# Layer norm's scale and shift, and four low parts of weights, move from GpSimd to VectorE; the inverse's matrix products leave out columns that are zero or finished

## The chip, the cores and the metric

The kernel runs on one core of one Trainium2 chip. The metric is the device time of one execution in microseconds (us); three runs of the kernel before were timed, and one more execution was profiled. The engines are called as the profile calls them: PE is TensorE (matrix products; PEld its weight loads), DVE is VectorE, ACT is ScalarE, POOL is GpSimd and SP is SyncE, whose queue starts most transfers.

## The reference

256 latent tokens and 256 context tokens of width 1024 pass through two layers of three sub-layers: a gated feed-forward half-step, a mixer, and a second half-step. Each ends in a layer norm with a scale row `g` and a shift row `b`.

```python
def layer_norm(x, g, b):
    mu = jnp.mean(x32, axis=-1, keepdims=True)
    var = jnp.mean(jnp.square(x32 - mu), axis=-1, keepdims=True)
    return ((x32 - mu) * lax.rsqrt(var + NORM_EPS) * g + b).astype(x.dtype)
...
def ffn_sublayer(x, m, s, w_gu, w_down, g, b):
    shift, scale, gate = _mod(m, s)
    y = swiglu(x * (1 + scale) + shift, w_gu, w_down)
    return layer_norm(DEEP_ALPHA * x + FFN_HALF * gate * y, g, b)
...
    lmat = jnp.where(strict, jnp.einsum('bnhid,bnhjd->bnhij', kb, kc) * decay, 0.0)
    rhs = jnp.concatenate([vc * bc[..., None], kb * jnp.exp(gc)[..., None]], axis=-1)
    uw = lax.linalg.triangular_solve(lmat, rhs, left_side=True, lower=True, unit_diagonal=True)
```

Layer 0's mixer joins windowed attention (A) with a gated delta rule (B), which needs the triangular solve above; layer 1's mixer (C) is dense attention with rotary positions. In layer 1 only the latent tokens go on after the mixer.

## The kernel before

**Sub-layers.** They are numbered 0 to 5: `ffn(0)`, `ab_proj` and what follows it (sub-layer 1, mixer A and B), `ffn(2)`, `ffn(3)`, `mixer_c` (sub-layer 4) and `ffn(5)`. The stream `x` lies as four row blocks of 128 tokens x 1024 (buffers `r`; two latent, two context). The norm at the end of a sub-layer is split. Mean and variance are taken out of the rows at once (`norm_tb`), and the next sub-layer's products read transposed rows into whose per-channel factors `g` and `b` are folded. The rows themselves, which the next residual sum reads, are multiplied by `g` and shifted by `b` later, in the next sub-layer, by `affine_tb`: one multiplication (line 326) and one addition (line 328) of 128x1024 for each row block, both on POOL. These are 8 instructions for each of sub-layers 0, 1 and 2, and 4 for each of 3 and 4 (latent rows only): 32. For sub-layer 3 they are put off (`deferred`) to slot 4 of the attention of `mixer_c`.

**Weights.** Products are made from two parts of each operand. For a 128x1024 piece of weights, ACT rounds the raw weights `wr` into the high part `wh` (line 366), and an engine subtracts to get the low part `wl` (line 368, `split_w`): DVE, except for 12 pieces on POOL, among them the four query pieces of `ab_proj` (`need`, jobs with `c0 < 1280`). Each product is three matmuls: lines 383, 385 and 386 (`mm3`).

**A chunk of a half-step.** `ffn` goes over 22 chunks of 128 hidden channels, in parts of 8, 8 and 6. A chunk is 48 matmuls into two banks `pgu`, 256 columns each in `ffn(5)`, 512 elsewhere. Then ACT takes the silu (`sg`), DVE multiplies `sg` by the other bank (line 432), ACT rounds (`hhi`) and DVE subtracts (`hlo`, line 434). `next_fill` adds DVE work of the modulation vectors behind it (`acc`, line 169).

**`ab_proj`.** The projections of q, k, v each go through `ab_conv`, a five-tap convolution: one tap on ACT (line 897), four on DVE (`cacc`, line 908). Lines 826 to 847 are `scalars`, small operations on 128x32. The rows are stored away to `xs` by two POOL transfers (line 997).

**The inverse.** `delta_inverse` solves the triangular systems as 8 units of four 128x128 blocks, in pairs: `begin` makes a product `pN` with the solved diagonal blocks `AT` (line 1390), ACT copies it to `N` (tile `va`, line 1394); three `step`s make `pZ` (line 1403) from `N` and subtract on DVE (line 1408). All run over 128 columns. The inverse is woven between the slots of mixer A's attention (products `pS`, `pP`, `pOa`; `qs` comes from POOL, line 1290).

The order on each engine is settled by a scheduler when the program is built; instructions then wait for each other across engines.

Of the kernel before, what the change touches and what calls it, by code (L numbers as in the profile page):

```python
# [32 lines left out]
class Backbone:  # L33
    def __init__(self, ctx, tc, io):
# [363 lines left out]
    def ffn(self, sub, tail, lat_only=False, fill=()):  # L398
# [238 lines left out]
    def boundary(self, sub, streams=(0, 1), affine=(0, 1)):  # L637
# [6 lines left out]
        def rows(last):  # L644
            self.load_ln(sub)

            def apply():
                for j in affine:
                    for tb in (2 * j, 2 * j + 1):
                        self.affine_tb(tb, last)  # L650

            if sub == 3:
                self.deferred = apply
            else:
                apply()
# [280 lines left out]
    def ab_proj(self):  # L936
# [952 lines left out]
```

## Time and profile before

| | us |
| --- | --- |
| runs, lowest / median / highest of 3 | 1824.44 / 1825.21 / 1827.54 |
| the profiled execution, its own time | 1826.35 |
| its span in the trace | 1824.6 |
| busy: PE / PEld / DVE / ACT / POOL | 1758.4 / 1484.9 / 1264.7 / 672.8 / 290.7 |

The profiled execution is one run of its own, 1.14 us above the median of the timed ones; 1.75 us of its time lie outside the span. Busy times count an engine's instructions and not its waits. The granted clock of PE, 0.987 of full speed over the span, is shown in the windows as a share of full speed: 1.00 is 2.4 GHz, 0.50 is 1.2 GHz.

### The profile page before, as it was taken

Reading aid. Unit: us, or ns where it says so; the run is one execution under the profiler, and the core shown is the slowest. Engines: PE = TensorE matmul, PEld = TensorE weight load, DVE = VectorE, ACT = ScalarE, POOL = GpSimd, SP = SyncE. Lnnn points to the kernel's source line nnn. Section 1 sums busy time; section 2 is a strip of 40 time slices with the busy share of each in tenths; the row PEclk is TensorE's granted clock in tenths of the full one; section 3 lists DMA queues with packets and bytes.
Section 4 is the critical chain, followed back from the end, with each engine's and each line's share of the span. In section 5 each row is a group of like instructions: output and inputs, shape, how many; then the busy total and the mean of one; then the engine's idle time right before and its main releaser. Section 6 shows DMA issues by size and latency. Waiting matters only on the chain. (4 is left out here: it accounts for less than half of the span.)

```text
span 1824.6 us, 24388 instructions
## 1 busy us (share of the span) xinstructions
PE 1758.4 (96%) x9571; PEld 1484.9 (81%) x9571; DVE 1264.7 (69%) x1912; ACT 672.8 (37%) x1178; POOL 290.7 (16%) x324
## 2 busy tenths in 40 slices
PE   6999999999998999999999999999999999999997
PEld 2978878878787888877887888778878888878997
DVE  2774855867688986896673438976747769786556
ACT  2432331324664662332221323423332335634442
POOL 1000000017433210510000003400000046150000
PEclk8999999999998999999999999999999999999999
DMA  9563553522341213375552242664644433136552
GB/s 349 185 216 128 185 182 120 197 59 95 127 116 54 75 59 104 128 240 187 162 184 70 93 154 77 212 204 141 204 163 139 155 108 113 59 126 232 186 177 99
DMA packets 178173, 267.56 MB, mean 147 GB/s; under 512 B 14639, under 2 KB 126683, under 8 KB 177547
## 3 DMA queue, kind: packets, MB, share of 16 engines
q1 hardware_dynamic: 172944, 250.58, 41.4%
q0 software_dynamic: 4624, 14.29, 2.4%
q8 instruction: 75, 1.23, 0.3%
q10 hardware_dynamic: 491, 1.15, 0.2%
q14 instruction: 39, 0.32, 0.1%
HBM read 259.64 MB, written 6.34 MB: 146 GB/s over the span
## 5 line engine op out<-in xcount | busy, mean ns | idle before, releaser
L366 ACT ACTIVATE wh<-wr 128x1024 fp32r<-128x1024 f32 (+1 forms) x311 | 324.8, 1056 | 756.7 <-PE pdn L386 306.6
L368 DVE TENSOR_TENSOR wl<-wr,wh 128x1024 fp32r<-128x1024 f32 (+1 forms) x299 | 390.0, 1315 | 231.9 <-ACT wh L366 228.5
L383 PE MATMUL pgu<-ht_hi,wh 128*128 128x512 f32 (+1 forms) x1472 | 519.5, 355 | 14.7 <-DVE sg L432 8.4
L386 PE MATMUL pgu<-ht_hi,wl 128*128 128x512 f32 (+1 forms) x1472 | 520.4, 354 | 3.3 <-DVE wl L368 3.3
L385 PE MATMUL pgu<-ht_lo,wh 128*128 128x512 f32 (+1 forms) x1472 | 520.6, 355 | 1.0 <-POOL ht_lo L268 0.5
L383 PEld LDWEIGHTS pgu<-ht_hi,wh 128*128 128x128 f32 x1472 | 279.1, 191 | 57.8 <-DVE sg L432 10.9
L386 PEld LDWEIGHTS pgu<-ht_hi,wl 128*128 128x128 f32 x1472 | 280.4, 191 | 41.6 <-DVE wl L368 3.9
L385 PEld LDWEIGHTS pgu<-ht_lo,wh 128*128 128x128 f32 x1472 | 280.5, 191 | 39.1 <-POOL ht_lo L268 0.9
L169 DVE SCALAR_TENSOR_TENSOR acc<-wa,cv,acc 128x1024 f32<-128x1024 f32 x224 | 277.1, 1299 | 0.0
L385 PE MATMUL pdn<-wl,hhi 128*128 128x512 f32 (+1 forms) x622 | 241.1, 388 | 0.0
L383 PE MATMUL pdn<-wh,hhi 128*128 128x512 f32 (+1 forms) x622 | 239.9, 389 | 0.0
L386 PE MATMUL pdn<-wh,hlo 128*128 128x512 f32 (+1 forms) x622 | 239.6, 388 | 0.0
L383 PEld LDWEIGHTS pdn<-wh,hhi 128*128 128x128 f32 x622 | 116.7, 188 | 27.6 <-issue 2.5
L385 PEld LDWEIGHTS pdn<-wl,hhi 128*128 128x128 f32 x622 | 116.9, 188 | 23.7
L386 PEld LDWEIGHTS pdn<-wh,hlo 128*128 128x128 f32 x622 | 116.9, 188 | 23.6
L432 DVE TENSOR_TENSOR sg<-sg,pgu 128x512 f32<-128x512 f32 (+1 forms) x86 | 53.6, 623 | 108.6 <-PE pgu L386 105.1
L615 DVE SCALAR_TENSOR_TENSOR tm<-pdn,gate 128x512 f32<-128x512 f32 (+1 forms) x98 | 64.3, 675 | 60.0 <-PE pdn L386 59.8
L197 POOL DMA_DIRECT2D gsc<-rows x12 | 6.2, 525 | 615.3 <-DVE rows L180 615.3
L433 ACT ACTIVATE hhi<-sg 128x512 fp32r<-128x512 f32 (+1 forms) x86 | 49.7, 577 | 89.4 <-DVE sg L432 89.3
L431 ACT ACTIVATE sg<-pgu 128x512 f32<-128x512 f32 (+1 forms) x86 | 45.9, 534 | 59.6 <-PE pgu L386 59.6
L434 DVE TENSOR_TENSOR hlo<-sg,hhi 128x512 fp32r<-128x512 f32 (+1 forms) x86 | 59.8, 695 | 7.7 <-ACT hhi L433 7.7
L318 POOL TENSOR_TENSOR mv<-mv,mhalf 128x1 f32<-128x1 f32 x18 | 16.6, 932 | 272.3 <-DVE mv L317 272.3
(385 smaller groups left out, 2351.3 us busy)
## 6 DMA issues: line engine op xcount, KB each, us to landing
wr<-in_ffn_w_gu_dram SPq DMA_DIRECT2D x84, 1024.0 KB
wa<-in_ada_w_dram SPq DMA_DIRECT2D x144, 512.0 KB
wr<-in_ffn_w_down_dram SPq DMA_DIRECT2D x40, 1024.0 KB
wr<-in_ab_w_in_dram SPq DMA_DIRECT2D x11, 1024.0 KB
wr<-in_c_w_in_dram SPq DMA_DIRECT2D x6, 1024.0 KB
gate<-gsc POOLq DMA_DIRECT2D x10, 512.0 KB, 4.5
wr<-in_ffn_w_gu_dram SPq DMA_DIRECT2D x8, 512.0 KB
wr<-in_ffn_w_down_dram SPq DMA_DIRECT2D x8, 512.0 KB
```

The costliest lines, as they stand in the source:

```text
L169: i = nc.vector.scalar_tensor_tensor(out=acc[:, sl], in0=wa[:, sl], scalar=cv, in1=acc[:, sl], op0=ALU.mult, op1=ALU.add)
L318: nc.gpsimd.tensor_tensor(out=mv[:, 3:4], in0=mv[:, 2:3], in1=self.mhalf[:, 0:1], op=ALU.pow)
L366: self.last_high = nc.scalar.activation(out=hv, in_=raw, func=AF.Copy)
L368: self.last_split = (eng or nc.vector).tensor_tensor(out=lv, in0=raw, in1=hv.bitcast(F32), op=ALU.subtract)
L383: self.first_mm = nc.tensor.matmul(out=out, lhsT=lhs[0], rhs=rhs[0], start=start, stop=False)
L385: self.link(nc.tensor.matmul(out=out, lhsT=lhs[0], rhs=rhs[1], start=False, stop=False))
L386: self.last_mm = nc.tensor.matmul(out=out, lhsT=lhs[1], rhs=rhs[0], start=False, stop=stop)
L431: nc.scalar.activation(out=sg, in_=pts[0][:, :NT], func=AF.Silu)
L432: nc.vector.tensor_tensor(out=sg, in0=sg, in1=pts[1][:, :NT], op=ALU.mult)
L433: nc.scalar.activation(out=h_hi[:, c, :], in_=sg, func=AF.Copy)
L434: self.evacuated = nc.vector.tensor_tensor(out=h_lo[:, c, :], in0=sg, in1=h_hi[:, c, :].bitcast(F32), op=ALU.subtract)
L615: i = nc.vector.scalar_tensor_tensor(out=tm, in0=pt[:, cs], scalar=mul, in1=self.gate[:, t // 2, ds], op0=ALU.mult, op1=ALU.mult)
```

## The change

- The 32 scale-and-shift instructions go from POOL to DVE. `affine_tb` now only lists them (`self.affine`), and `next_affine` issues them behind a named DVE instruction: sub-layer 0's 8, two behind each query convolution of `ab_proj`; sub-layer 1's and 2's 8, two behind each of chunks 2 to 5 of the next half-step; sub-layer 3's 4, one in each of slots 2 to 5 of the attention of `mixer_c`; sub-layer 4's 4, two behind each of chunks 2 and 3 of `ffn(5)`.
- The low parts of the four query pieces of `ab_proj` are made on DVE.
- The two stores to `xs` are issued behind query convolutions 1 and 3, and the tile `vt` is allocated later.
- In the inverse, `pN` is made over 96 columns, and the three `pZ` over 96, 64 and 32; the DVE subtraction and ACT's copy shrink alike, and Z is written straight into `AT`. POOL gains, for each unit, a `memset` of 32 columns of `N` and a copy of 32 columns into `AT`: 16 instructions.

```diff
     def affine_tb(self, tb, after):
         nc = self.nc
         x = self.row_block(tb)
-        i = nc.gpsimd.tensor_tensor(out=x, in0=x, in1=self.lnr[:, 0, :], op=ALU.mult)
-        self.after(i, [after])
-        nc.gpsimd.tensor_tensor(out=x, in0=x, in1=self.lnr[:, 1, :], op=ALU.add)
+        lnr = self.lnr
+
+        self.affine += [
+            lambda i=i: nc.vector.tensor_tensor(out=x, in0=x, in1=lnr[:, i, :], op=(ALU.mult, ALU.add)[i]) for i in range(2)
+        ]
+
+    def next_affine(self, n, behind):
+
+        for _ in range(min(n, len(self.affine))):
+            self.after(self.affine.pop(0)(), [behind])
...
             self.next_fill()
+            if n == 0 and c > 1:
+                self.next_affine(2, self.evacuated)
...
-                eng = nc.gpsimd if c0 < 1280 else None
-                ws.append(self.split_w(raws[p][:, :, c0 - p:c0 - p + P], bool(ext), eng))
+                ws.append(self.split_w(raws[p][:, :, c0 - p:c0 - p + P], bool(ext)))
...
             if h == 1:
                 rows()
+            self.next_affine(2, self.convolved)
+            if h % 2:
+                nc.gpsimd.dma_start(out=self.xs[:, h - 1:h + 1], in_=self.rows[h // 2])
...
+            c0 = 0 if u < 4 else 32
             pN = self.bank("sc", "pN")
+            p3 = pN[:, 0:384].rearrange("p (t x) -> p t x", t=4)
             for tb in range(4):
                 nc.tensor.matmul(
-                    out=pN[:, tb * P:(tb + 1) * P], lhsT=self.AT[u][:, tb, :], rhs=x[:, tb, :], start=True, stop=True
-                )
-            N = self.tmp("va")
-            i = nc.scalar.activation(out=N, in_=pN, func=AF.Copy)
+                    out=p3[:, tb, :], lhsT=self.AT[u][:, tb, :], rhs=x[:, tb, c0:c0 + 96], start=True, stop=True,
+                )
+
+            N = cube(self.tmp("va"))
+            i = nc.scalar.activation(out=N[:, :, c0:c0 + 96], in_=p3, func=AF.Copy)
+            zc = 96 if u < 4 else 0
+            nc.gpsimd.memset(N[:, :, zc:zc + 32], 0.0)
...
+            dc = 0 if u < 4 else 96
+            nc.gpsimd.tensor_copy(out=self.AT[u][:, :, dc:dc + 32], in_=xT[:, :, dc:dc + 32])
...
+            w = 96 - 32 * it
+            c0 = 128 - w if u < 4 else 0
+            Z = xT if it == 0 else self.AT[u]
...
-            Zn = self.AT[units[n]] if it == 2 else cube(self.tmp("o"))
-            V.tensor_tensor(out=Zn, in0=xT, in1=cube(pZ), op=ALU.subtract)
-            state[n] = (xT, N, Zn)
+                    out=p3[:, tb, :], lhsT=N[:, tb, :], rhs=Z[:, tb, c0:c0 + w], start=True, stop=True,
+                )
+            V.tensor_tensor(
+                out=self.AT[u][:, :, c0:c0 + w], in0=xT[:, :, c0:c0 + w], in1=p3, op=ALU.subtract
+            )
...
-            if i == 4:
-                self.deferred()
+            if 1 < i < 6:
+                self.next_affine(1, self.weighted)
```

The rows that follow show the order on two engines; line numbers of the changed kernel are up to 19 higher. First DVE in `ffn(2)`, chunks 2 to 4 of the first part (`sg` and `hlo` end a chunk, `acc` is the fill behind it), before:

```order
L432 TENSOR_TENSOR sg<-sg,pgu_6964 128x512
L368 TENSOR_TENSOR wl<-wr,wh 128x1024 x2
L434 TENSOR_TENSOR hlo<-sg,hhi 128x512
L169 SCALAR_TENSOR_TENSOR acc_6923<-wa,cv,acc_6923 128x1024 x2
L169 SCALAR_TENSOR_TENSOR acc_6924<-wa,cv,acc_6924 128x1024 x2
L432 TENSOR_TENSOR sg<-sg,pgu_7034 128x512
L368 TENSOR_TENSOR wl<-wr,wh 128x1024 x2
L434 TENSOR_TENSOR hlo<-sg,hhi 128x512
```

The same place of the changed kernel (line 376 is `wl`, 440 `sg`, 442 `hlo`, 170 `acc`):

```order
L440 TENSOR_TENSOR sg<-sg,pgu_6956 128x512
L376 TENSOR_TENSOR wl<-wr,wh 128x1024 x2
L442 TENSOR_TENSOR hlo<-sg,hhi 128x512
L170 SCALAR_TENSOR_TENSOR acc_6915<-wa,cv,acc_6915 128x1024 x2
L170 SCALAR_TENSOR_TENSOR acc_6916<-wa,cv,acc_6916 128x1024 x2
L330 TENSOR_TENSOR r_6318<-r_6318,lnr 128x1024
L440 TENSOR_TENSOR sg<-sg,pgu_7028 128x512
L376 TENSOR_TENSOR wl<-wr,wh 128x1024 x2
L330 TENSOR_TENSOR r_6318<-r_6318,lnr 128x1024
L442 TENSOR_TENSOR hlo<-sg,hhi 128x512
```

The chunk has gained two instructions of line 330, one ahead of the next `sg` and one ahead of the next `hlo`. Next POOL in `ab_proj`, from the last `ht_lo` (the low parts of the transposed rows) to the store, before:

```order
L268 TENSOR_TENSOR ht_lo<-h_3148,ht_hi 128x256
L326 TENSOR_TENSOR r_91<-r_91,lnr 128x1024 x2
L326 TENSOR_TENSOR r_92<-r_92,lnr 128x1024 x2
L1160 MEMSET X 128x1024
L328 TENSOR_TENSOR r_91<-r_91,lnr 128x1024
L368 TENSOR_TENSOR wl<-wr,wh 128x1024
L328 TENSOR_TENSOR r_91<-r_91,lnr 128x1024
L368 TENSOR_TENSOR wl<-wr,wh 128x1024
L328 TENSOR_TENSOR r_92<-r_92,lnr 128x1024
L368 TENSOR_TENSOR wl<-wr,wh 128x1024
L328 TENSOR_TENSOR r_92<-r_92,lnr 128x1024
```

And of the changed kernel:

```order
L269 TENSOR_TENSOR ht_lo<-h_3148,ht_hi 128x256
L1165 MEMSET X 128x1024
L1166 MEMSET X 128x32
L938 TENSOR_TENSOR rk<-ssk,mhalf 128x16
L938 TENSOR_TENSOR rki<-ssk,phalf 128x16
L1029 DMA xs<-r_91 128x2048
L1029 DMA xs<-r_92 128x2048
```

POOL has nothing of 128x1024 with an input left there; the eleven instructions stand on DVE. Last POOL in the inverse (`qs` feeds the attention scores, `xv` loads the next units), before:

```order
L1368 MEMSET xv 128x2048
L1290 TENSOR_TENSOR qs<-qTa,qs 64x128 x3
L1377 DMA xv<-scr_in 32x4x32 x8
L1290 TENSOR_TENSOR qs<-qTa,qs 64x128 x3
L1377 DMA xv<-scr_in 32x4x32 x2
L1290 TENSOR_TENSOR qs<-qTa,qs 64x128 x3
```

And of the changed kernel:

```order
L1373 MEMSET xv 128x2048
L1405 MEMSET va 128x4x32
L1295 TENSOR_TENSOR qs<-qTa,qs 64x128 x3
L1382 DMA xv<-scr_in 32x4x32 x8
L1295 TENSOR_TENSOR qs<-qTa,qs 64x128 x3
L1410 COPY AT<-xv 128x4x32
L1405 MEMSET va 128x4x32
L1382 DMA xv<-scr_in 32x4x32
L1410 COPY AT<-z 128x4x32
L1382 DMA xv<-scr_in 32x4x32
L1295 TENSOR_TENSOR qs<-qTa,qs 64x128 x2
```

The `COPY` and `MEMSET` of a unit now stand ahead of some `qs` and `xv` in one queue.

## Rows read from the trace of the kernel before

**Rows 1.** The page of the profile: busy time of each engine, share of the span, instructions.
```profile
PE 1758.4 (96%) x9571; PEld 1484.9 (81%) x9571; DVE 1264.7 (69%) x1912; ACT 672.8 (37%) x1178; POOL 290.7 (16%) x324
```

**Rows 2.** The list of waits, engine PE, whole span: total us, times, longest us.
```profile
PE pgu L383 <- DVE sg L432: 8.4, 6, 2.0
...
PE pcT L1707 <- DVE kTlo L1712: 2.0, 1, 2.0
```

**Rows 3.** Groups by line and shape, DVE, 760 to 784 us: busy us, mean ns.
```profile
L368 DVE TENSOR_TENSOR wl<-wr,wh 128x1024 fp32r<-128x1024 f32 x4 | 12.9, 3268 | 0.0
L434 DVE TENSOR_TENSOR hlo<-sg,hhi 128x512 fp32r<-128x512 f32 x2 | 4.4, 2201 | 0.7 <-ACT hhi L433 0.7
...
L432 DVE TENSOR_TENSOR sg<-sg,pgu 128x512 f32<-128x512 f32 x2 | 1.3, 674 | 0.0
```

**Rows 4.** The same view, DVE, 805 to 840 us.
```profile
L169 DVE SCALAR_TENSOR_TENSOR acc<-wa,cv,acc 128x1024 f32<-128x1024 f32 x17 | 20.8, 1284 | 0.0
L368 DVE TENSOR_TENSOR wl<-wr,wh 128x1024 fp32r<-128x1024 f32 x8 | 9.7, 1224 | 0.0
...
L434 DVE TENSOR_TENSOR hlo<-sg,hhi 128x512 fp32r<-128x512 f32 x4 | 2.8, 689 | 0.0
```

**Rows 5.** The instructions of line 326: ns, first and last start.
```profile
L326 POOL TENSOR_TENSOR r<-r,lnr x16: 2405/2516/3384, 434.9 to 1629.7; 128x1024 f32<-128x1024 f32 x16
```

**Rows 6.** The timeline in sub-layer 2, PE: start us, length us, instruction.
```profile
797.19 0.51 PE L383 MATMUL pgu<-ht_hi,wh 128*128 128x512 f32 x1 [2.04 <-DVE sg L432]
...
798.50 0.63 PE L386 MATMUL pgu<-ht_hi,wl 128*128 128x512 f32 x1
...
801.89 0.40 PE L385 MATMUL pgu<-ht_lo,wh 128*128 128x512 f32 x1
...
802.59 0.40 PE L385 MATMUL pgu<-ht_lo,wh 128*128 128x512 f32 x1
```

**Rows 7.** The list of waits, engine PE, 1132 to 1190 us.
```profile
PE pgu L383 <- DVE sg L432: 3.9, 3, 2.0
```

**Rows 8.** The timeline in the query projections of `ab_proj`, DVE, ACT and PE.
```profile
457.25 2.42 DVE L834 TENSOR_SCALAR beta<-beta 128x32 f32<-128x32 f32 x1
...
460.25 1.79 DVE L830 SCALAR_TENSOR_TENSOR gu<-gy 128x32 f32<-128x32 f32 x1
...
462.07 0.23 ACT L831 ACTIVATE gu<-gu 128x32 f32<-128x32 f32 x1 [3.54 <-DVE gu L830]
...
464.91 0.66 PE L917 MATMUL pqt<-ident,sqT 128*128 128x128 f32 x4 [0.94 <-ACT sqT L912]
...
470.47 0.51 PE L383 MATMUL pproj<-ht_hi,wh 128*128 128x512 f32 x1 [3.32 <-ACT cacc L897]
```

**Rows 9.** Busy us by stretch: PE, PEld, DVE, ACT, POOL, clock, DMA share, GB/s.
```profile
460.00:480.00 20.00, 15.74 (x73) 12.79 (x72) 14.50 (x39) 11.85 (x37) 8.98 (x6) 0.91 0.60 211
600.00:640.00 40.00, 39.18 (x335) 35.27 (x334) 36.54 (x113) 26.98 (x87) 9.23 (x19) 1.00 0.25 84
1625.00:1645.00 20.00, 16.56 (x103) 14.66 (x102) 16.66 (x15) 6.73 (x12) 13.06 (x8) 0.91 0.21 63
```

**Rows 10.** The list of waits, engine PE, 1625 to 1665 us.
```profile
PE pgu L386 <- DVE wl L368: 3.3, 3, 2.3
PE pgu L383 <- ACT wh L366: 1.4, 1, 1.4
PE plead L386 <- DVE ht_lo L299: 0.8, 1, 0.8
```

**Rows 11.** The timeline of PE: a 128-column product of the inverse, a 32-column product.
```profile
591.28 1.06 PE L1403 MATMUL pZ<-o,va 128*128 128x128 f32 x8
592.09 0.48 PE L1298 MATMUL pS<-kk,qs 128*128 128x256 f32 x2
...
477.73 0.39 PE L859 MATMUL pgc<-gg,ones 128*128 128x32 f32 x2
477.95 0.64 PE L917 MATMUL pqt<-ident,sqT 128*128 128x128 f32 x4
```

More of the change, by code (lines that the diff above doesn't have):

```diff
@@ L46, in __init__ @@
         self.turn_at = 0
+        self.affine = []
     def new_ht(self):
@@ L645, in rows @@
             self.load_ln(sub)
[L647 to L655, printed above, removed]
+            for j in affine:
+                for tb in (2 * j, 2 * j + 1):
+                    self.affine_tb(tb, last)
         def context():
@@ L995, in ab_proj @@
         self.start_context()
-        for j in range(2):
-            nc.gpsimd.dma_start(out=self.xs[:, 2 * j:2 * j + 2], in_=self.rows[j])
         for n in range(4):
@@ L1039, in ab_proj @@
             self.ab_gram(h)
+            if h == 0:
+                self.vt = L.tile([P, 4, 4, P], F32, tag="gate", name="vt", bufs=1)
         self.ab_pow(self.rq, ssq, -0.5)
@@ L1387, in begin @@
             xT, x = (a, bt) if u < 4 else (bt, a)
+            c0 = 0 if u < 4 else 32
             pN = self.bank("sc", "pN")
+            p3 = pN[:, 0:384].rearrange("p (t x) -> p t x", t=4)
             for tb in range(4):
                 nc.tensor.matmul(
-                    out=pN[:, tb * P:(tb + 1) * P], lhsT=self.AT[u][:, tb, :], rhs=x[:, tb, :], start=True, stop=True
+                    out=p3[:, tb, :], lhsT=self.AT[u][:, tb, :], rhs=x[:, tb, c0:c0 + 96], start=True, stop=True
                 )
-            N = self.tmp("va")
-            i = nc.scalar.activation(out=N, in_=pN, func=AF.Copy)
+            N = cube(self.tmp("va"))
+            i = nc.scalar.activation(out=N[:, :, c0:c0 + 96], in_=p3, func=AF.Copy)
+            zc = 96 if u < 4 else 0
+            nc.gpsimd.memset(N[:, :, zc:zc + 32], 0.0)
             if n == 7:
                 self.mark = i
-            state[n] = (xT, N, xT)
+            dc = 0 if u < 4 else 96
+            nc.gpsimd.tensor_copy(out=self.AT[u][:, :, dc:dc + 32], in_=xT[:, :, dc:dc + 32])
+            state[n] = (xT, N)
         def step(n, it):
-            xT, N, Z = state[n]
+            u = units[n]
+            xT, N = state[n]
+            w = 96 - 32 * it
+            c0 = 128 - w if u < 4 else 0
+            Z = xT if it == 0 else self.AT[u]
             pZ = self.bank("sc", "pZ")
+            p3 = pZ[:, 0:4 * w].rearrange("p (t x) -> p t x", t=4)
             for tb in range(4):
                 nc.tensor.matmul(
-                    out=pZ[:, tb * P:(tb + 1) * P], lhsT=N[:, tb * P:(tb + 1) * P], rhs=Z[:, tb, :],
-                    start=True, stop=True,
-                )
-            Zn = self.AT[units[n]] if it == 2 else cube(self.tmp("o"))
-            V.tensor_tensor(out=Zn, in0=xT, in1=cube(pZ), op=ALU.subtract)
-            state[n] = (xT, N, Zn)
+                    out=p3[:, tb, :], lhsT=N[:, tb, :], rhs=Z[:, tb, c0:c0 + w], start=True, stop=True,
+                )
+            V.tensor_tensor(
+                out=self.AT[u][:, :, c0:c0 + w], in0=xT[:, :, c0:c0 + w], in1=p3, op=ALU.subtract
+            )
         jobs = []
@@ L1758, in scores @@
             V.reciprocal(out=st[:, 3:4], in_=st[:, 2:3])
-            V.tensor_scalar(out=pe, in0=pe, scalar1=st[:, 3:4], scalar2=None, op0=ALU.mult)
+            self.weighted = V.tensor_scalar(out=pe, in0=pe, scalar1=st[:, 3:4], scalar2=None, op0=ALU.mult)
             state[i] = pe
```

3 lines of the change are left out of this document (1 added, 2 removed).

## The prediction

> **What bounds the kernel now.** I read the page's busy times first: PE works 1758.4 us of a span of 1824.6, DVE 1264.7, POOL 290.7 [rows 1]. PE is the bound, so the change can win in two ways only: PE's 66 us of idle time and of its slower clock, or products made shorter. The second view is the list of what PE waited for. Its largest group is PE waiting for DVE's `sg`, 8.4 us in six waits [rows 2]; all six lie in `ffn(2)` and `ffn(3)`, 3.9 us of them in the latter [rows 7]. So the question is why DVE is late there, although it is busy for only 69% of the span.
>
> The third view answers it: DVE's instructions by shape, in two stretches of `ffn(2)`. From 760 to 784 us, while POOL runs its eight scale-and-shift instructions, one `wl` takes 3268 ns and one `hlo` 2201 [rows 3]. From 805 to 840 us, with POOL idle, they take 1224 and 689 [rows 4]. The stretched `wl` is about as long as one of POOL's instructions, 2405 to 3384 ns [rows 5]. `sg` of line 432, which reads one of its inputs from a PSUM bank, is not stretched: 674 ns beside POOL's work [rows 3], where the same-sized `hlo` tripled. So a DVE instruction with both inputs in SBUF waits out a POOL instruction of this kind. The Trainium skill states the same in "SBUF — State Buffer", section "Who interferes with whom", and this trace agrees with it; the sum below needs only the rows.
>
> What a PE wait costs beyond itself is seen in the timeline: behind the wait of 2.04 us at 797.19, eight products take from 798.50 to 801.89, 3.39 us, where three take 0.70 us afterwards, 0.233 each [rows 6]. The granted clock is at the lower of its two levels there, and that costs 3.39 - 8 x 0.233 = 1.5 us more. The windows show the same loss twice again: the clock averages 0.91 in 460 to 480 us and in 1625 to 1645 us [rows 9], 1.8 us of full clock each, which I count as 1.5 too. In `ffn(3)` no such loss followed.
>
> **The change part by part.**
>
> *`ffn(2)`.* DVE loses the stretching: 4 x (3.268 - 1.224) + 2 x (2.201 - 0.689) = 11.2 us in that one stretch [rows 3, 4]. It gains eight instructions of 128x1024 with two SBUF inputs. No such DVE instruction with this operation stands in the trace; the nearest is `wl`, same shape, 1.224 us [rows 4], which I take since POOL is idle there: 9.8 us in all. The ends are nothing, and 3.3 us each, as `wl` beside POOL; the latter only if POOL still worked there. They come later, though, behind chunks 2 to 5, and the first `sg` that PE waited 2.04 us for stands ahead of all of them. It is 11 us earlier and PE can want it at most 3 us earlier. From then on a chunk costs DVE four `acc` (5.1), two `wl` (2.4), `sg` and `hlo` (1.4) and two new ones (2.4): 11.3 us [rows 3, 4], against 48 x 0.233 = 11.2 us of PE [rows 6]. Four such chunks in a row are level, on a lead of some 8 us. So all three waits go: 8.4 - 3.9 = 4.5 us [rows 2, 7], and the clock's 1.5: **6.0**. Bound from below: none gained, if the chunks fall behind.
>
> *`ffn(3)`.* The same work and order; 3.9 us of waits [rows 7], no clock loss: **3.9**, lower bound again 0.
>
> *`ab_proj`.* DVE's `beta` and `gu` on 128x32, small things, take 2.42 and 1.79 us beside POOL, ACT stands 3.54 us for `gu`, and ACT is then late with `sqT` and `cacc`, for which PE waits 0.94 and 3.32 us [rows 8]. With the clock that is 5.8 us. POOL leaves, but DVE takes eight instructions of 1.2 us and four `wl` of 1.2: 14.7 us in a stage where it was busy 14.5 of 20 us with POOL still in the way [rows 9]. For one head it then has four taps, a `wl`, two scale-and-shifts and small work, some 6.7 us (1.224 us for the 128x1024 ones [rows 4], 0.7 a tap as for `sg`, which has its size and one input in PSUM [rows 3]), against 24 x 0.233 = 5.6 us of PE and some transposes. PE will wait for taps to free the bank. I take half: **3**; bounds 0 and 5.8. The stores carry rows that are read after the mixer: nothing. But the second one waits on POOL's queue for the last of the eight, and behind it stand the queries' norm power and the products `sqT`; if that one is late, so are they, which is in the half that I leave out.
>
> *`mixer_c`.* `kTlo` comes 2.0 us late in a stage where POOL scales and shifts [rows 2]. That goes; in exchange four score slots each get 1.2 us of DVE. Full cover would cost nothing, none 4.9 us; the slots before ran without waits of this size, so I take a loss of 1: **1**, bounds -2.9 and 2.0.
>
> *`ffn(5)`.* 3.3 for `wl`, 0.8 for `ht_lo`, 1.4 for a `wh` (whose transfer was issued behind a late `wl`) [rows 10], and the clock's 1.5 [rows 9]: 7.0. DVE keeps two `wl` and gets two new instructions in each of two chunks that last 48 x 0.12 = 5.6 us on PE at 256 columns (half of 0.233): tight, and the `wh` may remain: **6**, bounds 3 and 7.
>
> *The inverse.* Eight 128-column records of the inverse take 0.81 us from 591.28 to the next product at 592.09: 0.10 each. Two records of a 32-column product take 0.22 us from 477.73 to 477.95: 0.11 each [rows 11]. Fewer columns did not make a record shorter. There are 8 units x 16 products x 2 records = 256 of them, 26 us. If columns counted, the sum would fall by 1 - (96 + 96 + 64 + 32)/512 = 0.44, 11 us; by the row it falls by **0**, and I take the row. The Trainium skill, "TensorE: Matmul & The Clock Gate", section "LDWEIGHTS (loading the stationary operand)", has a weight load go by the columns of the weights, about 107 ns for 128, whatever the product's width; by that the gain is nothing too. Its section "Back-to-back issue gap" gives a gap that grows with the product's columns; by it alone my estimate of the gain would be 256 x (128 - 72)/2.4 ns, 6 us. DVE's and ACT's shorter instructions save time that PE covers: PE is busy 39.18 of 40 us here, DVE 36.54, at clock 1.00 [rows 9]. POOL gets 16 more instructions in front of `qs`; it is busy 9.23 of 40 us [rows 9], so they fit, unless they wait.
>
> The sum: 6.0 + 3.9 + 3 + 1 + 6 + 0 = 19.9 us. From the profiled execution's 1826.35 us that leaves 1806.4; it ran 1.1 us above the median, so against the runs shown **1805 us**. With every term at its upper bound (24.7) it would be 1800; with `ab_proj` at 0, `mixer_c` at -2.9 and `ffn(5)` at 3, 1815.
>
> **The rivals.** *The narrow products pay.* For it: products shorter by 44% of their columns. Against it: [rows 11]. 1805 - 11 = 1794 us.
>
> *The stalls come back through a full DVE.* At 11.3 against 11.2 us a chunk, one late weight transfer at the start would use up the lead, and in `ab_proj` DVE is over PE's pace. If each half-step keeps half of its gain and `ab_proj` and `mixer_c` none, the gain is 3.0 + 2.0 + 0 + 0 + 4 = 9: 1816 us.
>
> *Nothing changes.* The waits would be set by weights landing late, and DVE's lateness only lie beside them. For it: the `wh` wait [rows 10]. Against it: the other waits end with a DVE instruction that stretched. 1825 us.
>
> *Slower: POOL's queue in the inverse.* The copy into `AT` cannot run before the unit's four `pN` products have read `AT`, and the `memset` not before the earlier unit has left its buffer. Behind them on the same queue stand `qs`, which the scores need, and the `xv` transfers of the next pair. If PE waits for `qs` or `pZ` at each of the eight units, and loses 1.5 us of clock behind each wait, a wait of 1.5 us gives 24 us and a tie; from 2 us each it is slower than before: 1829 us. Against it: PE had hardly a gap there, and POOL three quarters of its time free [rows 9].
>
> **How the numbers follow.** The forecast has 0.57, its own range 1800 to 1812; narrow products that pay 0.12; stalls that return 0.17; nothing changes 0.08; slower 0.06. A change under 0.2%, 3.7 us, can hardly be told from none on this kernel. Faster is 0.57 + 0.12 + 0.17 = 0.86, the same 0.08, slower 0.06. The range takes in the rivals at 1794 and 1816, with the bounds around them: 1790 to 1819.
>
> **What would show it.** Right: no `sg` wait of PE above 0.5 us in `ffn(2)` and `ffn(3)`; `wl` and `hlo` at 1.2 and 0.7 us throughout; the new line at 1.2 us; the clock at 1.00 in 790 to 840 us of the old time; PE's time in the inverse as before, at 0.10 to 0.11 a record. Wrong: `sg` waits in chunks 3 to 6, a wait for `qs` or for the new `memset`, a record at 32 columns much shorter than 0.10, or a clock below 1.00 in the inverse.

## The result, and the profile after

The changed kernel takes **1804.86 us** (median of four executions, 1803.61 to 1809.13); the kernel before took 1825.97 beside it (four, 1824.44 to 1827.54). The ratio is 0.9888, its 95% interval 0.9869 to 0.9907. The profiled execution took 1804.25 us, its span 1802.5.

The page's busy times after, beside [rows 1]:

```profile
PE 1755.9 (97%) x9571; PEld 1481.4 (82%) x9571; DVE 1239.9 (69%) x1948; ACT 670.2 (37%) x1176; POOL 196.8 (11%) x304
```

PE's work is 2.5 us shorter and its instructions are as many. The span is 22.1 us shorter. So nearly all of the gain is idle time that is gone.

The list of waits of the changed kernel, engine PE, whole span, beside [rows 2] (total us, times, longest):

```profile
PE pP L1329 <- DVE pexp L1322: 3.6, 2, 3.3
...
PE pgu L391 <- ACT h L266: 3.5, 1, 3.5
PE pqt L921 <- ACT sqT L916: 3.1, 1, 3.1
```

No group of `sg`, `kTlo` or `wl` is left in it. The wait for `sqT` has grown from 0.94 to 3.1 us, and the one for `cacc`, 3.32 us before [rows 8], has become 0.2. One more wait is gone, which the kernel before had at the start of `ffn(2)` (its list of waits, PE, 730 to 1110 us):

```profile
PE pgu L383 <- DVE tm L615: 1.9, 1, 1.9
```

Groups by line and shape, DVE, 805 to 830 us of the changed kernel: chunks of `ffn(2)` into which the new line 330 was put (busy us, mean ns):

```profile
L170 DVE SCALAR_TENSOR_TENSOR acc<-wa,cv,acc 128x1024 f32<-128x1024 f32 x10 | 12.2, 1278 | 0.0
L330 DVE TENSOR_TENSOR r<-r,lnr 128x1024 f32<-128x1024 f32 x5 | 6.1, 1217 | 0.0
L376 DVE TENSOR_TENSOR wl<-wr,wh 128x1024 fp32r<-128x1024 f32 x5 | 5.9, 1217 | 0.0
L442 DVE TENSOR_TENSOR hlo<-sg,hhi 128x512 fp32r<-128x512 f32 x3 | 2.0, 683 | 0.0
```

The new instruction takes 1217 ns, as `wl` beside it, and `acc`, `wl` and `hlo` stand where they stood with POOL idle [rows 4]. Not only instructions with two inputs in SBUF had been held up: `beta`, which has one input of 128x32 and a constant, took 2.42 us [rows 8] while POOL made one of the query `wl` (457.24 to 459.63 us). The timeline of DVE in the changed kernel:

```profile
462.21 0.17 DVE L838 TENSOR_SCALAR beta<-beta 128x32 f32<-128x32 f32 x1
```

Three stretches of the changed kernel (busy us of PE, PEld, DVE, ACT, POOL, clock, DMA share, GB/s):

```profile
460.00:480.00 20.00, 16.71 (x85) 13.97 (x84) 19.46 (x42) 13.60 (x53) 8.50 (x3) 0.91 0.29 105
600.00:640.00 40.00, 39.60 (x346) 35.79 (x347) 32.43 (x111) 27.40 (x89) 10.24 (x25) 1.00 0.25 83
785.00:835.00 50.00, 50.00 (x222) 41.39 (x221) 50.00 (x48) 15.07 (x20) 0.00 (x0) 1.00 0.60 203
```

In 785 to 835 us both PE and DVE are busy for 50.00 of 50 us, at clock 1.00: level, as worked out, and nothing waits. The clock's average of 0.91 in `ab_proj` has stayed [rows 9].

To see where the time came from, the program is cut at PE's first transposes (`ptr`) of each sub-layer, so that the same work lies between two borders. The view of stretches, of the kernel before, sub-layers 1 to 5 in order:

```profile
403.80:733.00 329.20, 316.00 (x2113) 275.09 (x2112) 255.89 (x635) 174.61 (x456) 108.94 (x144) 0.98 0.28 88
733.00:1108.30 375.30, 368.42 (x1736) 305.05 (x1734) 239.47 (x266) 108.24 (x133) 39.59 (x31) 1.00 0.45 149
1108.30:1485.90 377.60, 373.19 (x1773) 307.98 (x1772) 273.14 (x299) 113.34 (x138) 46.60 (x42) 1.00 0.48 160
1485.90:1609.50 123.60, 115.59 (x798) 105.74 (x797) 103.37 (x233) 71.18 (x184) 47.88 (x39) 0.97 0.35 116
1609.50:1824.60 215.10, 197.78 (x1351) 182.99 (x1349) 135.79 (x184) 87.66 (x126) 26.38 (x23) 0.98 0.48 159
```

And of the changed kernel:

```profile
403.90:731.50 327.60, 315.99 (x2113) 275.15 (x2112) 250.46 (x647) 171.80 (x454) 86.41 (x148) 0.98 0.28 88
731.50:1100.10 368.60, 368.34 (x1736) 303.85 (x1735) 233.34 (x274) 108.31 (x133) 15.60 (x23) 1.00 0.45 152
1100.10:1475.00 374.90, 374.63 (x1774) 307.98 (x1773) 267.49 (x307) 113.37 (x138) 22.66 (x34) 1.00 0.49 161
1475.00:1596.40 121.40, 115.22 (x798) 104.59 (x797) 100.11 (x238) 71.85 (x184) 36.15 (x35) 0.99 0.35 118
1596.40:1802.50 206.10, 194.52 (x1351) 181.25 (x1349) 131.48 (x187) 87.31 (x126) 14.62 (x19) 0.98 0.49 166
```

The first column is the length, the second PE's busy time; the difference is what PE stood still.

| us | length | PE standing still | PE busy | forecast |
| --- | --- | --- | --- | --- |
| sub-layer 1 (`ab_proj`, mixers A and B, inverse) | -1.6 | 13.2 to 11.6 | 0.0 | -3 |
| `ffn(2)` | -6.7 | 6.9 to 0.3 | -0.1 | -6.0 |
| `ffn(3)` | -2.7 | 4.4 to 0.3 | +1.4 | -3.9 |
| sub-layer 4 (`mixer_c`) | -2.2 | 8.0 to 6.2 | -0.4 | -1 |
| `ffn(5)` | -9.0 | 17.3 to 11.6 | -3.3 | -6 |
| sum | -22.2 | | | -19.9 |

The sum is close, but the terms are off by 0.7 to 3 us, in both directions. The experiments ask why.

One caution first. In a second profiled execution of the same changed kernel (span 1806.6 us; more of it below), `ffn(2)` and `ffn(3)` take the same 368.5 and 374.9 us, `mixer_c` 122.1 and `ffn(5)` 206.7. Sub-layer 1, however, is longer than in the kernel before:

```profile
403.30:734.30 331.00, 318.40 (x2113) 277.16 (x2112) 250.85 (x647) 171.81 (x454) 85.84 (x148) 0.97 0.27 87
```

So a gain in sub-layer 1 is not shown; its row differs by 3.4 us between two executions of one kernel. With this profile the five rows sum to -17.5 us. The other four rows hold within 0.7 us.

### The profile page after: what moved, and what is told of

It reads as the page before. It is cut to its first block, busy times and chain, and to the rows that moved or that the text cites. A ratio compares the mean times of both kernels' runs of the same rounds, so it can differ in the third digit from the quotient of the medians.

```text
span 1802.5 us, 24408 instructions
## 1 busy us (share of the span) xinstructions
PE 1755.9 (97%) x9571; PEld 1481.4 (82%) x9571; DVE 1239.9 (69%) x1948; ACT 670.2 (37%) x1176; POOL 196.8 (11%) x304
## 5 line engine op out<-in xcount | busy, mean ns | idle before, releaser
L376 DVE TENSOR_TENSOR wl<-wr,wh 128x1024 fp32r<-128x1024 f32 (+1 forms) x303 | 367.7, 1225 | 225.3 <-ACT wh L374 222.0
L170 DVE SCALAR_TENSOR_TENSOR acc<-wa,cv,acc 128x1024 f32<-128x1024 f32 x224 | 272.7, 1278 | 0.0
L442 DVE TENSOR_TENSOR hlo<-sg,hhi 128x512 fp32r<-128x512 f32 (+1 forms) x86 | 53.6, 623 | 12.2 <-ACT hhi L441 12.2
L393 PE MATMUL pproj<-ht_lo,wh 128*128 128x512 f32 (+1 forms) x160 | 55.7, 352 | 0.0
```

Source lines behind the costliest of these rows:

```text
L170: i = nc.vector.scalar_tensor_tensor(out=acc[:, sl], in0=wa[:, sl], scalar=cv, in1=acc[:, sl], op0=ALU.mult, op1=ALU.add)
L376: self.last_split = (eng or nc.vector).tensor_tensor(out=lv, in0=raw, in1=hv.bitcast(F32), op=ALU.subtract)
L393: self.link(nc.tensor.matmul(out=out, lhsT=lhs[0], rhs=rhs[1], start=False, stop=False))
L442: self.evacuated = nc.vector.tensor_tensor(out=h_lo[:, c, :], in0=sg, in1=h_hi[:, c, :].bitcast(F32), op=ALU.subtract)
```

## The experiments

**Theory:** a DVE instruction that reads two operands from SBUF is held up by a POOL instruction that reads SBUF too; taking POOL out of these stages takes the stretching and PE's waits away, and the narrow inverse is worth nothing. **Rivals:** it is the later place of the scale-and-shift work that counts and not its engine; or the narrow products carry part of the gain; or DVE's new load costs something that hides in the sum.

### The parts alone

The kernel before with the scale-and-shift work on DVE and the later stores, the query `wl` left on POOL, the inverse unchanged:

```diff
-                eng = nc.gpsimd if c0 < 1280 else None
-                ws.append(self.split_w(..., bool(ext), eng))
+                ws.append(self.split_w(..., bool(ext), nc.gpsimd if c0 < 1280 else None))
...
+            if n == 0 and c > 1:
+                self.next_affine(2, self.evacuated)
```

> The kernel before with one part of the change alone: the 32 scale-and-shift instructions on DVE, with the stores to xs behind them; the four query low parts stay on POOL, the inverse stays 128 columns wide. Theory (PE waits came from DVE instructions that wait out POOL's scale-and-shift): nearly the whole gain of the change, 17 to 22 us, so 1804 to 1809 us, with no sg wait of PE over 0.5 us in ffn(2) and ffn(3). Rival (the shorter products of the inverse carry a third or more of the gain): 1813 us or more here.

Measured: 1819.4 us (1816.98 to 1821.0), ratio 0.9957 (0.9944 to 0.9969). That misses the expectation by 10 us. `ffn(3)` (374.9 us) and `ffn(5)` (206.8, against 206.1) took about as long as in the changed kernel, and no `sg` wait was left. But sub-layer 1 took 334.4 us. The list of waits of this kernel, PE, 500 to 760 us:

```profile
PE pS L1303 <- POOL qs L1295: 8.0, 1, 8.0
...
PE pgu L391 <- DVE tm L625: 3.1, 1, 3.1
```

Both look like matters of order; that was not shown by itself. The last record of the products `pG`, which DVE's recurrence needs before it starts, begins at 529.2 us here, at 523.7 before and at 522.4 in the changed kernel; the recurrence starts at 542.5 us, against 535.8 and 535.2, and PE waits 8.0 us for `qs` behind it, 1.2 us in both other kernels. And the `tm` that PE needs at the start of `ffn(2)` comes 3.1 us late, with the clock at 0.93 on average in 735 to 760 us (1.00 in the changed kernel).

The kernel before with the narrow inverse alone:

```diff
-                    out=pN[:, tb * P:(tb + 1) * P], lhsT=self.AT[u][:, tb, :], rhs=x[:, tb, :], start=True, stop=True
+                    out=p3[:, tb, :], lhsT=self.AT[u][:, tb, :], rhs=x[:, tb, c0:c0 + 96], start=True, stop=True
...
+                    out=p3[:, tb, :], lhsT=N[:, tb, :], rhs=Z[:, tb, c0:c0 + w], start=True, stop=True,
```

> The kernel before with the narrow inverse alone, POOL's 16 new instructions included. Theory (a record of a product takes about 0.11 us whatever its columns): 1825 us, plus or minus 2, and PE's time in the inverse as before. Rival (columns count): 11 us less, 1814 us. Second rival (POOL's memset and copy hold up qs): 1828 us or more.

Measured: 1827.41 us (11 executions, 1825.64 to 1829.72), ratio 1.0006 (0.9998 to 1.0015): neither gain nor loss, as by theory. The timeline of PE in the inverse of the changed kernel, a product of 96 columns and one of 32 (start, length):

```profile
610.91 1.03 PE L1423 MATMUL pZ<-xv,va 128*128 128x96 f32 x8
611.77 0.38 PE L1329 MATMUL pP<-ident,pexp 128*128 128x128 f32 x2
...
616.34 0.98 PE L1423 MATMUL pZ<-AT,va 128*128 128x32 f32 x8
617.15 0.71 PE L1303 MATMUL pS<-kk,qs 128*128 128x512 f32 x2
```

Eight records take 0.86 us to the next product at 96 columns and 0.81 at 32, where 128 columns took 0.81 [rows 11]. The record spacing does not fall with the columns, and PE's busy time in sub-layer 1 is 316.0 us before and in the changed kernel.

The changed kernel with the wide inverse put back, the same edit the other way round:

```diff
-                    out=p3[:, tb, :], lhsT=self.AT[u][:, tb, :], rhs=x[:, tb, c0:c0 + 96], start=True, stop=True
+                    out=pN[:, tb * P:(tb + 1) * P], lhsT=self.AT[u][:, tb, :], rhs=x[:, tb, :], start=True, stop=True
```

> The changed kernel with the inverse wide again: 128 columns in every product, no memset and no copy on POOL there. Theory (a record costs the same whatever its columns, and DVE's and ACT's savings there are covered by PE): 1805 us, plus or minus 3. Rival (the inverse is what affine_only lacked of the gain): 1815 us or more. If it is near 1805, what affine_only lacked lies with the four query low parts, or with the order that the scheduler gave it.

Measured: 1813.06 us (1812.03 to 1814.78), ratio 0.9921 (0.9908 to 0.9933), 8 us above the changed kernel by the medians, 6 by the ratios: a miss. By the rival of narrow products this loss would lie in the inverse. Sub-layer 1 took 328.4 us, though, against 327.7. The larger part lies in `ffn(2)`, 373.0 us against 368.5, whose list of waits (PE, 500 to 760 us) has the wait that the changed kernel has lost:

```profile
PE pgu L391 <- DVE tm L625: 3.1, 1, 3.1
```

The inverse is finished by then. Each of these builds puts the `tm` work of DVE in another place; before, PE waited 1.9 us for it, in the changed kernel not at all. So some microseconds of the result belong to an order that no line of the change asks for, and the parts do not add up: about 0 us for the narrow inverse and -7 for the moved scale-and-shift work alone, -21 together. A third part is in neither: the four query low parts on DVE. This kernel and `affine_only` differ in nothing else, and this one is the faster, 0.9921 against 0.9957; 6.0 us of that lie in sub-layer 1 (328.4 against 334.4), where PE's wait for `qs` is 1.2 us again and not 8.0. Whether it is POOL's reading or once more the order that makes this part worth so much was not tried, nor why the scheduler chose each order.

### Engine or place

The changed kernel with the scale-and-shift instructions back on POOL:

```diff
-            lambda i=i: nc.vector.tensor_tensor(out=x, in0=x, in1=lnr[:, i, :], op=(ALU.mult, ALU.add)[i]) for i in range(2)
+            lambda i=i: nc.gpsimd.tensor_tensor(out=x, in0=x, in1=lnr[:, i, :], op=(ALU.mult, ALU.add)[i]) for i in range(2)
```

> The changed kernel, with the 32 scale-and-shift instructions at their new places but on POOL again. Theory (the engine counts, since a DVE instruction with two SBUF inputs waits out a POOL one): wl, hlo and acc beside them in ffn(2) at 2 to 3.4 us again; DVE's chunk grows from 8.9 us by the stretching of some 3 us, over PE's 11 us at times, so part of the waits return: 1808 to 1818 us. Rival (only the place counts, behind the chunks and not ahead of them): 1805 us, as the changed kernel.

Measured: 1834.32 us (1833.51 to 1838.66), ratio 1.0045 (1.0032 to 1.0057), 16 us above the range expected. The timeline of POOL in `ffn(2)` says why this run doesn't tell engine from place:

```profile
764.63 24.01 POOL L330 TENSOR_TENSOR r<-r,lnr 128x1024 f32<-128x1024 f32 x8
```

All eight ran in one piece from 764.63 us, where they ran before. "Behind" is an order on one engine only; across engines it makes no instruction wait. So `wl` took 2126 ns on average in 755 to 805 us, `sg` made PE wait 12.3 us in six waits, and the edit was made again with a real wait:

```diff
+            i = self.affine.pop(0)(self.nc.gpsimd if pool else self.nc.vector)
+            if pool:
+                self.tc.add_manual_dep(
+                    i.ins, behind.ins.name,
+                    mybir.DependencyInfo(mybir.DependencyClass.Sync, mybir.DependencyReason.DATA),
+                    reason="behind the chunk",
+                )
...
-                self.next_affine(2, self.evacuated)
+                self.next_affine(2, self.evacuated, sub in (2, 3))
```

> The changed kernel, with the sixteen scale-and-shifts of ffn(2) and ffn(3) on POOL, each pair held by a real wait until its chunk's hlo is done, so that they run at the new place and not at the old one; the others stay on DVE. Theory (the engine counts): wl and acc beside them take 2.4 us or more again, DVE's chunk grows from 8.9 us to 12 or more, over PE's 11, and after the lead of some 8 us is used up PE waits for sg again, 1 to 3 us in each half-step. Rival (the place counts, since a late pair finds DVE with slack): the instructions may stretch but PE does not wait, and ffn(2) with ffn(3) take no longer than with the pada products together, 738.5 us from the first transposes of ffn(2) to those of sub-layer 4.

Measured: 1824.2 us (11 executions, 1821.74 to 1830.13), ratio 0.9987 (0.9974 to 0.9999). The place is that of the changed kernel, and the gain is gone: `ffn(2)` and `ffn(3)` together take 760.3 us, against 743.4 in the changed kernel and 752.9 in the kernel before. PE's waits in this kernel, whole span:

```profile
PE pada L137 <- DVE acc L170: 8.8, 2, 4.4
...
PE pgu L399 <- DVE sg L448: 5.8, 5, 1.4
```

The `sg` waits are back, and the late `acc` now holds up `pada`.

Groups by line and shape, 795 to 850 us, DVE:

```profile
L170 DVE SCALAR_TENSOR_TENSOR acc<-wa,cv,acc 128x1024 f32<-128x1024 f32 x19 | 40.3, 2176 | 0.0
L384 DVE TENSOR_TENSOR wl<-wr,wh 128x1024 fp32r<-128x1024 f32 x9 | 10.8, 1211 | 0.0
```

and POOL:

```profile
L330 POOL TENSOR_TENSOR r<-r,lnr 128x1024 f32<-128x1024 f32 x7 | 23.0, 3291 | 16.8 <-DVE hlo L450 11.7 <-issue 4.7
```

`acc` is stretched from 1278 to 2176 ns on average. `wl` keeps its 1.2 us here, unlike what was expected: POOL's pairs start at 791.4, 804.0, 815.4 and 828.0 us, each as DVE begins four `acc`. POOL's own instruction, 2405 ns at the least and 2516 in the median before [rows 5], takes 3291 on average: both sides lose. It is the engine, and the place does not save it. The Trainium skill says in "SBUF — State Buffer", section "Who interferes with whom", that a DVE instruction with two SBUF inputs contends with a POOL instruction that reads SBUF, and not with one that only writes it; the two stretched rows agree with the first half, and the run that follows with the second.

The other end is a POOL that is just as busy but reads nothing. The kernel before, with 24 `memset` in place of sub-layer 1's eight instructions:

```diff
+                if sub == 1:
+                    for i in range(24):
+                        k = self.nc.gpsimd.memset(self.lnr[:, i % 2, :], 0.0)
+                        self.after(k, [last])
+                    return
```

> The kernel before, with sub-layer 1's eight scale-and-shifts in ffn(2) left out; in their place POOL runs 24 memsets of 128x1024, some 23 us, which write SBUF and read nothing. ffn(3) is as before, as a control. Theory (a DVE instruction waits out a POOL instruction that reads SBUF): wl at 1.2 us beside the memsets, no sg wait over 0.6 us in ffn(2), 6 us less, 1820 us, while ffn(3) keeps its 3.9 us of waits. Rival (any POOL instruction on SBUF does it): wl at 1.9 us or more beside them, and waits in ffn(2) as before.

The profiled execution took 1817.76 us. Its timeline on POOL in `ffn(2)`, then DVE's groups in 755 to 783 us:

```profile
758.82 21.74 POOL L650 MEMSET lnr<- 128x1024 f32 x24
```

```profile
L368 DVE TENSOR_TENSOR wl<-wr,wh 128x1024 fp32r<-128x1024 f32 x7 | 8.3, 1222 | 0.3 <-ACT wh L366 0.3
...
L434 DVE TENSOR_TENSOR hlo<-sg,hhi 128x512 fp32r<-128x512 f32 x2 | 1.4, 688 | 3.3 <-ACT hhi L433 3.3
```

`wl` takes 1222 ns and `hlo` 688 beside 21.74 us of `memset`, against 3268 and 2201 beside the scale-and-shift work [rows 3]. `ffn(2)` took 368.0 us without an `sg` wait; `ffn(3)`, left as it was, still waited 2.6 us for `sg` and took 377.6. So POOL's being busy and its writing are not enough; what the `memset` lacks is the reading. Whether one input would do, where the scale-and-shift work has two, was not tried. The other four executions of this kernel took 1840.2 to 1842.0 us (ratio of all five 1.0075), at a mean clock of 0.982 to 0.984 against 0.988, and there is no trace of them; I rest only on the profiled one, and what the others lost stays open.

### What DVE's new load costs

The kernel before without the 16 scale-and-shift instructions in `ffn(2)` and `ffn(3)`:

```diff
-            else:
+            elif sub not in (1, 2):
                 apply()
```

> The kernel before, with the sixteen scale-and-shifts in ffn(2) and ffn(3) left out, POOL idle there. Theory: the waits of 4.5 and 3.9 us and the clock's 1.5 go, 10 us, so 1816 us; the pada products stay side by side, so each of the two half-steps is 2 us shorter than in the changed kernel. Rival (the waits come from weights landing late): 1822 us or more.

Measured: 1814.64 us (1812.45 to 1815.71), ratio 0.9927 (0.9913 to 0.9941); `ffn(2)` 367.8 us and `ffn(3)` 372.2. With the work on DVE the changed kernel has 368.5 and 374.9. So 3.4 us are lost somewhere when DVE takes it over, although no wait of PE shows it. They are in PE's busy time, where the loss is even larger: 365.6 to 368.3 us in `ffn(2)` and 371.9 to 374.6 in `ffn(3)`, 5.4 in all, since `ffn(2)` without the work still has the wait of 1.9 us for `tm` that the changed kernel has lost. The timeline of PE before, at the end of the first part of `ffn(2)`, where the sums `acc` are multiplied into `pada`:

```profile
839.32 1.92 PE L136 MATMUL pada<-acc,pick 128*32 128x512 f32 x16
841.17 0.51 PE L383 MATMUL pdn<-wh,hhi 128*128 128x512 f32 x1
```

And of the changed kernel:

```profile
835.89 1.05 PE L137 MATMUL pada<-acc,pick 128*32 128x512 f32 x4
836.88 0.50 PE L391 MATMUL pdn<-wh,hhi 128*128 128x512 f32 x1
```

`pada` are products of 32 columns of weights, four of them on different columns of the array. Before, all 16 records (half of them in each of two rounds) stand together and take 1.85 us to the next product. After, they stand in four groups of four with `pdn` between, and each group takes 0.98 to 0.99 us: 3.94 in all, 2.1 more. The Trainium skill, "TensorEngine Tiling (Array Packing)", section "Key Properties", says that such tiles work independently and can run at the same time; the 16 records in 1.85 us agree, since a record of 512 columns takes 0.23 us by itself [rows 6] and 16 of them would take 3.7. Split up they lose it. No group waited for its sum: the timeline of DVE in the changed kernel has the last four `acc` done at 833.56 us, 2.3 us ahead of the first group.

```profile
828.69 4.87 DVE L170 SCALAR_TENSOR_TENSOR acc<-wa,cv,acc 128x1024 f32<-128x1024 f32 x4
```

So the split lies in the order that the scheduler had settled for PE. A likely reason is that the scheduler reckoned with sums that become ready one by one; that was not shown by itself.

So the products were made to wait for the last of the sums, in the changed kernel:

```diff
+                for o in hold:
+                    self.tc.add_manual_dep(
+                        i.ins, o.ins.name,
+                        mybir.DependencyInfo(mybir.DependencyClass.Sync, mybir.DependencyReason.DATA),
+                        reason="sums complete",
+                    )
...
+                    state["summed"] = i
...
-                    product(self.pick[:, j, :], state["acc"][j], j == 0, j == 1)
+                    product(self.pick[:, j, :], state["acc"][j], j == 0, j == 1, [state["summed"]])
```

> The changed kernel, with the eight pada products of each group of modulation vectors made to wait for the last of their sums, so that the scheduler puts them one behind the other, as before, and not in four pairs between pdn products. Theory (four neighbouring pada products on 32 columns each run side by side, 16 records in 1.85 us before, and pairs of them took 0.98 us each, 3.9 in all): 2 us less in each of ffn(2) and ffn(3), so some 4 us under the changed kernel, 1801 us. Rival (the place of pada does not matter, PE lost the 2 us elsewhere): 1805 us.

Measured: 1803.01 us (1800.99 to 1807.05), ratio 0.9865 (0.985 to 0.988). The intervals of this kernel and of the changed one overlap, so both ran again beside each other:

> The changed kernel itself once more, beside the two kernels that follow, so that they can be compared on one chip: 1805 us, plus or minus 2.

> The changed kernel with the pada products together, again. Theory: ffn(2) and ffn(3) 4.9 us shorter than in the changed kernel, as in its first profile, and the rest as it falls out of the scheduler: 1800 to 1803 us. Rival: no difference that lasts, 1805 us.

Measured: 1808.92 us for the changed kernel (1804.29 to 1809.99), ratio 0.9891 (0.9871 to 0.9911); 1805.07 with `pada` together (1801.76 to 1806.27), ratio 0.9877 (0.9858 to 0.9895). `ffn(2)` and `ffn(3)` took 743.4 and 738.4 us, as in the first runs of each (743.4 and 738.5). Both whole times came out above what was expected. The timeline of PE with `pada` together:

```profile
841.09 1.92 PE L137 MATMUL pada<-acc,pick 128*32 128x512 f32 x16
842.94 0.50 PE L401 MATMUL pdn<-wh,hlo 128*128 128x512 f32 x1
```

1.85 us again, and 5.0 us over both half-steps, which is repeatable by stage; over the whole time it is blurred by sub-layer 1, which takes 327.7 to 331.0 us in the four profiles of these two kernels, in part by the clock. Here is one stretch of the changed kernel's second profile, in sub-layer 1:

```profile
620.00:650.00 30.00, 29.60 (x226) 26.92 (x224) 22.66 (x71) 18.65 (x54) 5.17 (x11) 0.89 0.10 36
```

The clock averages 0.89 there; in the first profile of the same kernel it was 1.00. In 455 to 480 us it is the other way round, 1.00 in the second and 0.93 in the first, with the same wait of 3.1 us for `sqT` in both. With `pada` together `ffn(3)` takes the 372.2 us that it takes without the scale-and-shift work, `ffn(2)` 366.2, and no wait of PE in either is above 0.3 us: DVE's eight instructions of 1217 ns cost nothing in each.

### The query projections

The prediction held that DVE is full in `ab_proj`. The changed kernel without sub-layer 0's eight instructions:

```diff
-            for j in affine:
+            for j in affine if sub else ():
```

> The changed kernel with sub-layer 0's eight scale-and-shifts left out, so that DVE has 9.8 us less in ab_proj. The prediction's theory (half of the gain there is lost because DVE is full): PE's wait of 3.1 us goes, 1801 us. Rival (that wait is ACT's, which makes squares, a high part and two table loads ahead of sqT): it stays at 3 us, and the time at 1805.

Measured: 1808.36 us (1807.62 to 1808.98), ratio 0.9894 (0.988 to 0.9907). PE's wait there:

```profile
PE pqt L921 <- ACT sqT L916: 3.2, 1, 3.2
```

The same as with them (3.1). Yet DVE had much less to do, 14.80 us in this stretch where it had 19.46 with them (length, then busy us of PE, PEld, DVE, ACT and POOL):

```profile
460.00:480.00 20.00, 16.84 (x88) 14.43 (x87) 14.80 (x39) 13.16 (x52) 5.81 (x2) 0.91 0.17 53
```

So DVE is not what is late. Sub-layer 1 took 324.3 us, 3.4 less than in the changed kernel's first profile, but PE stood still for the same 11.6 us; the difference is in PE's busy time and no larger than that between two executions of the changed kernel. The whole time gained nothing, since `ffn(2)` took 373.1 us, with the wait of 3.1 us for `tm`. The timeline of the changed kernel at that place, ACT and then PE (in brackets the wait):

```profile
464.64 1.12 ACT L374 ACTIVATE wh<-wr 128x1024 fp32r<-128x1024 f32 x1
465.78 1.28 ACT L916 ACT_TABLE_LOAD   x1
467.07 0.63 ACT L916 ACTIVATE sqT<-cacc 128x512 f32<-128x512 f32 x1
...
467.76 0.76 PE L921 MATMUL pqt<-ident,sqT 128*128 128x128 f32 x4 [3.14 <-ACT sqT L916]
```

ACT makes a `wh`, then loads a table for 1.28 us, then makes `sqT` from `cacc` (a silu); from 454 us on it has no gap. It is ACT's queue. The next run put DVE's and ACT's earlier small work behind the first query convolution, on top of `pada` together:

```diff
-        k_tok(3)
-        V.tensor_scalar(out=ssk, in0=ssk, scalar1=EPS, scalar2=None, op0=ALU.add)
-        self.ab_pow(rk, ssk, -0.5)
-        self.ab_pow(rki, ssk, 0.5)
...
             if h == 0:
+                k_tok(3)
+                V.tensor_scalar(out=ssk, in0=ssk, scalar1=EPS, scalar2=None, op0=ALU.add)
+                self.ab_pow(rk, ssk, -0.5)
+                self.ab_pow(rki, ssk, 0.5)
```

> The kernel with the pada products together, and the last key head's transposes and squares in ab_proj issued behind the first query convolution, not ahead of it, so that ACT has four copies and squares less ahead of the first sqT. Theory (PE's wait of 3.1 us there is ACT's backlog): the wait under 1.5 us, the clock's 1.5 us after it gone, 2 to 4 us under the kernel with pada together. Rival (the wait is the table load and the taps themselves): the wait stays at 3 us, no difference.

Measured: 1803.59 us (1799.45 to 1804.21), ratio 0.9862 (0.9843 to 0.988). Its ratio is the lowest of all, but within the interval of the run without this edit; ACT's order ahead of `sqT` did not change and the wait is 3.2 us. What an earlier `sqT` would bring stays open.

## Why the prediction was right, and where its steps were off

- **Stretching of DVE by POOL: right.** `wl` and `hlo` are at 1.2 and 0.7 us, the new line at 1.2, no `sg` wait is left, and with POOL reading at the same places the waits and the time come back.
- **`ffn(2)`, 6.0 forecast, 6.7 measured.** The 4.5 us of `sg` waits went as said. The 1.9 us for `tm`, which the sum did not have, went too, by the scheduler's order; and the clock's 1.5 us were eaten by `pada`, 2.1 us, which the sum did not have either. Two unforeseen terms of opposite sign.
- **`ffn(3)`, 3.9 forecast, 2.7 measured.** The 3.9 us of waits went; PE's busy time grew by 1.4 through the split `pada`. Put together, the stage gave 5.4.
- **`ab_proj`, 3 forecast, 1.6 for the whole of sub-layer 1 in the first profile and -1.8 in the second.** The step that failed is "DVE is over PE's pace" as the reason why half is lost: DVE was nearly full (19.46 of 20 us), but without the new instructions the wait was the same. The `cacc` wait went (3.32 to 0.2), and `sqT` took its place (0.94 to 3.1), late by ACT and its table load. So 1.0 us of waits was won and the clock's loss stayed; in the second profile the loss was not there, but PE waited 1.1 us for DVE's `cacc`, the one sign of a full DVE.
- **`mixer_c`, 1 forecast, 2.2 measured (1.5 in the second profile).** `kTlo` went (2.0), and the slots' new DVE work cost nothing: its upper bound, not the loss of 1 that was taken.
- **`ffn(5)`, 6 forecast, 9.0 measured.** The waits listed before sum to 6.7 us and 0.6 is left; PE stands still 5.7 us less, where 5.5 of the estimate of 7.0 were waits; the `wh` wait went with the others, so the 1 us taken off for it was not needed. PE's busy time fell by 3.3 us, where 1.5 was taken for the clock. The clock was sized rightly: 16 products at the lower level of the clock (1.2 GHz) take from 1634.71 to 1638.12 us, 3.41, against 16 x 0.12 = 1.9, so 1.5. What the sum lacked is what each wait costs beside its idle time. The last product ahead of a wait counts as busy for its whole 0.28 us, and the first behind it takes 0.22 to the next, where a product in the flow takes 0.12; such products make up nearly all of the remaining 1.8 us (rows below).
- **The inverse, 0 forecast: right**, within about 1 us either way (1.0006 alone). The slower rival failed as well: PE's wait for `qs` is 1.2 us before and after. That rival's own sum was off: 24 us lost against 19.9 won is 4 us slower and no tie, which is its 1829; with 2 us each it would have been 1833.

The timeline of PE before in `ffn(5)`, at both ends of the slow products and on both sides of the `wh` wait:

```profile
1634.71 0.41 PE L385 MATMUL pgu<-ht_lo,wh 128*128 128x256 f32 x1
...
1638.12 0.28 PE L386 MATMUL pgu<-ht_hi,wl 128*128 128x256 f32 x1
...
1646.53 0.28 PE L386 MATMUL pgu<-ht_hi,wl 128*128 128x256 f32 x1
1648.16 0.39 PE L383 MATMUL pgu<-ht_hi,wh 128*128 128x256 f32 x1 [1.35 <-ACT wh L366]
1648.38 0.28 PE L385 MATMUL pgu<-ht_lo,wh 128*128 128x256 f32 x1
```

So 19.9 against 22.2 us of span (17.5 with the second profile) is partly luck: `ffn(5)` and `mixer_c` gave more, `ab_proj` and `ffn(3)` less, and what the scheduler did to `tm` and `pada` partly cancelled.

## What to carry to other kernels

When DVE instructions that read two SBUF operands take 1.7 to 3.2 times what the same shape takes elsewhere, look for a POOL instruction that reads SBUF beside them, and give that work to DVE if DVE has the time: 1.2 us there cost less than 2.4 to 3.3 us on POOL. After an edit that changes when operands become ready, compare PE's order too, since products that ran side by side may have been split without any wait showing it. And under a scheduler, judge a part of a change by its stage, not by the difference of two whole times: here `ffn(2)` came out 4.4 us longer after an edit of the inverse alone. Profile the same kernel twice before a difference of a few microseconds is believed: sub-layer 1 differed by 3.4 us between two executions.

## What the runs showed of the hardware that I had not expected

- POOL pays for the contention too: its scale-and-shift instruction took 3291 ns on average beside DVE's `acc`, 2405 at the least in the kernel before.
- A DVE instruction with one input of 128x32 (`beta`) took 2.42 us beside a 128x1024 `wl` on POOL, and 0.17 with POOL idle.
- 24 `memset` on POOL, 21.74 us without a gap, left a DVE `wl` at 1222 ns.
- 16 `pada` records took 1.85 us in one piece and 3.94 in four.
- Eight records of the inverse took 0.81 us at 128 and at 32 columns, and 0.86 at 96.
- The granted clock fell in one execution of a kernel and not in another at the same place: 0.89 and 1.00 in 620 to 650 us, with PE busy for 29.60 us in both; and 1.00 and 0.93 in 455 to 480 us, with the same wait of 3.1 us.
- The last product ahead of a wait of PE and the first behind it cost 0.28 and 0.22 us of busy time, where one in the flow takes 0.12.
